# Attention in a two-layer decoder trunk: the causal mask added by rounded fp32 matmuls, a pair's first two blocks turned in one go, the head norms' small transposes held until the next turning

## Chip, core and metric

One core of one Trainium2 chip runs the whole program. The time is device microseconds from start to end of one execution; the kernel before was run three times, with a median of 1141.16 us. The engines are named as the profile names them: PE (TensorE matmul), PEld (its weight loads), DVE (VectorE), ACT (ScalarE), POOL (GpSimd), SP (the queue that issues most DMAs).

## What is computed

Two layers over 512 tokens of width 1024. The first has the attention that the change touches: 16 heads of width 64, 8 with forgetting attention (fox) and 8 with stick-breaking attention. Cut to that:

```
q, k, v = heads of rms_norm(h) @ w_in;   q, k = rms_norm(q), rms_norm(k)   # per head
# fox heads
logits = q k^T * 64**-0.5 + cum_f[query] - cum_f[key];  logits = -inf where key > query
o_fox  = softmax(logits) @ v
# stick-breaking heads
z = q k^T * 64**-0.5;  w = exp(log_sigmoid(z) + sum of log_sigmoid(-z) over later keys), strictly causal
o_sb   = w @ v
h = h + concat(o_fox, o_sb) @ w_out
```

A gated convolution mixer in the second layer and an MLP in each layer follow; the change leaves them alone.

## The kernel before

Nearly all matmuls take fp32 numbers split in two rounded halves (`hi`, and `lo`, the rest), and a product is three matmuls, hi·hi, hi·lo and lo·hi (lines 271 to 273 for the projections, 527 to 529 for the values). Each weight chunk that arrives (`raw`) is split by one ACT copy (L250) and one DVE subtraction (L251).

Heads go in 8 pairs `p` of two heads `e`; pairs 0 to 3 are fox, 4 to 7 stick-breaking. Query blocks of 128 rows go in three units: blocks 0 and 1 together, block 2, block 3 (`UNITS`). For each pair and unit:

- `logits` (L623): the **score** matmuls (L645). Head 0 lies in rows 0 to 63 of the PE array and head 1 in rows 64 to 127, each with its own PSUM bank of tag `b` (four buffers, shared with the projections). For fox pairs a fourth group with `dl` and `dr` adds the decay, and then **the mask** is added (L654): an identity matrix times a 128x128 mask, both bf16, over all 128 rows of the array. Softmax (L662 to 668) or sigmoids and a scan (L683 to 689) give the weights `w`.
- `turn` (L694): one unit later, **the turning**: transposes of 128x128 on PE into a PSUM bank of tag `c` (two buffers); L705 for blocks 0 and 1, L717 for blocks 2 and 3. ACT copies the bank to `pt` hi (L711, L720) and DVE takes the rest (L712, L721), which frees the bank.
- `weigh` (L724), when a pair's last block is turned: `w @ v` on PE (L741), then L747 and L748 join the two heads.

Between these, `fill` runs pieces of **fillers**: generators that yield matmuls of the following pairs' projections (`queries_keys`, L545), of the values, and at last of the output projection (L752, L766).

A pair's head norm is a chain of small steps off the projections, each put off by some us of planned PE time with `after` (L190) and started by `spend` (L185), which adds up planned time and runs what has come due: **sums** (L564, sums of squares over a head, matmuls 32 columns wide in the array, into a `c` bank), **turned_sums** (L572, two transposes in the same bank, which is free only after L574), the reciprocal roots on DVE (L356 to 368), and **rows** (L597, two times four transposes into two `c` banks; DVE multiplies at L599, L372 and L373 split the result into `qk_hi`, `qk_lo`). The scores of that pair need it (`need`, L540).

The order in which the program issues its instructions comes from a scheduler behind the tile framework: it takes the code's order as a wish and moves instructions of an engine where its own estimate finds the operands late. So a change in when steps are called moves rows on all engines.

Of the kernel before, what the change touches and what calls it, by code (L numbers as in the profile page):

```python
# [17 lines left out]
F32 = mybir.dt.float32  # L18
F32R = mybir.dt.float32r
# [6 lines left out]
P = 128  # L26
S = 512
# [16 lines left out]
ORDER = (1, 0, 1, 1, 1, 1, 3)  # L44
SUMS, FLAT, ROWS = 3.0, 1.5, 8.0
NSUMS, NROWS, LATE = 4.0, 3.0, 7.0
FILL1, FILL2, BEFORE = 1.5, 3.3, 2.0
UNITS = (0, 1), (2,), (3,)
CLASSIC = 3
SHARE = 0.58  # L50
# [3 lines left out]
def trunk(  # L54
# [7 lines left out]
    act, dve, pe, pool = nc.scalar, nc.vector, nc.tensor, nc.gpsimd  # L62
# [10 lines left out]
    def bank(tag):  # L73
        n_ps[0] += 1
        return ps.tile([P, S], F32, tag=tag, name=f"ps{tag}{n_ps[0]}", bufs={"a": 2, "b": 4, "c": 2}[tag])
# [52 lines left out]
    ident16 = begin[:, S - P:S]  # L128
    make_identity(nc, ident16)
    mask = const.tile([P, P], BF16, tag="mask", name="mask")  # L130
# [51 lines left out]

    clock, later, fillers, quota = [0.0], [], [], [0.0]

    def spend(us):  # L185
        clock[0] += us
        while later and later[0][0] <= clock[0]:
            later.pop(0)[2]()

# [8 lines left out]
    def fill(us):  # L198
        quota[0] += us
        while quota[0] > 0 and fillers:  # L200
            before = clock[0]
            if next(fillers[0], None) is None:
                fillers.pop(0)
            quota[0] -= clock[0] - before
# [240 lines left out]
    def choose():  # L445

        one = const.tile([P, 4, 4], F32, tag="one", name="one")
        pool.memset(one, 0.0)
        for j in range(4):
            for e in range(2):  # L450
                pool.affine_select(
                    out=one[:, j, :], in_=one[:, j, :], pattern=[[-1, 4]], compare_op=ALU.not_equal,
                    fill=1.0, base=-(e * HD + 4 * j), channel_multiplier=1,
                )
        both = const.tile([P, 2, 4], F32, tag="both", name="both")
        pool.tensor_tensor(both, one[:, 0::2, :], one[:, 1::2, :], op=ALU.add)
        two = const.tile([P, 4, 2], F32, tag="two", name="two")
        pool.tensor_tensor(two, one[:, :, 0:2], one[:, :, 2:4], op=ALU.add)
        by = const.tile([P, 4], F32, tag="by", name="by")
        pool.tensor_tensor(by, two[:, :, 0], two[:, :, 1], op=ALU.add)  # L460
        cols = const.tile([P, 4], F32, tag="cols", name="cols")
        pool.tensor_tensor(cols[:, 0:2], by[:, 0:2], by[:, 2:4], op=ALU.add)
        pool.tensor_tensor(cols[:, 2:4], by[:, 0::2], by[:, 1::2], op=ALU.add)
        pool.tensor_scalar(cols[:, 3:4], cols[:, 3:4], -1.0, None, op0=ALU.mult)
        sel = {n: cols[:, i:i + 1] for i, n in enumerate(("hi", "lo", "q", "-k"))}
        for p in range(4):
            sel["q", p], sel["k", p] = (both[:, i, p:p + 1] for i in range(2))
        return sel
# [71 lines left out]
    def need(what):  # L540
        while what not in done:
            assert fillers
            fill(0.5)
# [75 lines left out]
    def at_once(u):  # L619

        return (slice(0, 2),) if u == 0 else (slice(0, 1), slice(1, 2))

    def logits(p, u):  # L623


        fox = p < 4
        need(("qk", p))
        need("decay")
        (k_hi, k_lo), (q_hi, q_lo) = (halves[p][i] for i in range(2))
        bs = UNITS[u]  # L630
        ss = [bank("b") for _ in range(2)]

        parts, at_ = [], 0
        for i, b in enumerate(bs):
            n = (b + 1) * P
            parts.append((b, n, 256 * i, at_))
            at_ += n
            spend((4 if fox else 3) * max(n, 256) * 0.00044 + (0.12 if fox else 0))

        def scores(ql, kl, first, last):  # L640
            for b, n, c, _ in parts:
                wide = max(n, 256)
                for e in range(2):
                    rows = slice(e * HD, (e + 1) * HD)
                    pe.matmul(ss[e][:, c:c + wide], ql[rows, b * P:n], kl[rows, 0:wide], start=first and b == bs[0], stop=last and b == bs[-1])  # L645

        scores(q_hi, k_hi, True, False)
        scores(q_hi, k_lo, False, False)
        scores(q_lo, k_hi, False, not fox)
        if fox:  # L650
            scores(dl[:, p, :], dr, False, False)
            for e in range(2):
                for b, n, c, _ in parts:
                    pe.matmul(ss[e][:, c + b * P:c + n], ident16, mask, start=False, stop=b == bs[-1])  # L654
        w = aw.tile([P, 2, S], F32, tag="w", name=f"w{p}{u}", bufs=2)
        own = [w[:, :, a:a + n] for b, n, c, a in parts]
        if fox:
            m = len(bs)
            top, total, inv = (tiny.tile([P, m, 2], F32, tag=f"{t}{m}", name=f"{t}{p}{u}") for t in ("top", "total", "inv"))
            for j, (b, n, c, a) in enumerate(parts):  # L660
                for e in range(2):
                    dve.reduce_max(top[:, j, e:e + 1], ss[e][:, c:c + n], axis=AX.X, negate=True)  # L662
                    act.activation(own[j][:, e, :], ss[e][:, c:c + n], AF.Exp, bias=top[:, j, e:e + 1], accum_out=total[:, j, e:e + 1])
            for es in at_once(u):
                dve.reciprocal(inv[:, :, es], total[:, :, es])
                for j in range(m):
                    for e in range(es.start, es.stop):
                        dve.tensor_scalar(own[j][:, e, :], own[j][:, e, :], inv[:, j, e:e + 1], None, op0=ALU.mult)
        else:

            scale = q_scale[p]
            if not rests:
                rests.append(aw.tile([P, 2, S + 1], F32, tag="rest", name="rest", bufs=1))
                pool.memset(rests[0][:, :, S:S + 1], 0.0)
            rest = rests[0]
            if u == 0:
                pool.memset(rest[:, :, P:P + 1], 0.0)
            for es in at_once(u):
                for j, (b, n, c, a) in enumerate(parts):
                    end = P if b == 0 else S  # L680
                    keys = slice(end - n, end)
                    for e in range(es.start, es.stop):
                        act.activation(rest[:, e, keys], ss[e][:, c:c + n], AF.Sigmoid, scale=scale[:, 1, b, e:e + 1])  # L683
                        act.activation(own[j][:, e, :], ss[e][:, c:c + n], AF.Sigmoid, scale=scale[:, 0, b, e:e + 1])
                        back = rest[:, e, keys][:, ::-1]
                        dve.tensor_tensor_scan(back, back, begin[:, S - n:S][:, ::-1], 0.0, op0=ALU.mult, op1=ALU.max)  # L686
                for j, (b, n, c, a) in enumerate(parts):
                    end = P if b == 0 else S
                    dve.tensor_tensor(own[j][:, es], own[j][:, es], rest[:, es, end - n + 1:end + 1], op=ALU.mult)
        return [(b, x) for (b, n, c, a), x in zip(parts, own)]  # L690
# [87 lines left out]
    def output_begin():  # L778
        last_w.append([weights(), weights(AHEAD - 1)])
        yield from output_part(range(4), range(2), "b")  # L780
        last_w.append([weights(AHEAD - 1), weights(0)])
        yield from output_part(range(4), (2,), "b")
# [96 lines left out]
    aw = attn.enter_context(tc.tile_pool(name="aw", bufs=2))  # L879
# [4 lines left out]
    o_tiles = {0: mixed(0)}  # L884

    dl = ap_.tile([P, 4, S], F32R, tag="dl", name="dl")
    dr = aw.tile([P, 2, S + 1], F32, tag="rest", name="dr", bufs=1)[:, 0, 0:S].bitcast(F32R)
    sel = choose()
    run(qk0)
    load_small()  # L890
# [7 lines left out]
    units = [(p, u) for p in range(8) for u in range(len(UNITS))]  # L898
    waiting = {}
    fill(PRE)  # L900
    for g in range(len(units) + 2):
        if g < len(units):
            waiting[g] = logits(*units[g])
            fill(FILL1)
        if g == len(units):
            fillers.append(output_begin())
            fill(BEFORE)
        if g >= 2 and units[g - 2][1] == len(UNITS) - 1:
            p = units[g - 2][0]
            weigh(p)  # L910
            if p == 3:
                fillers.append(output(0, residual))
        if 1 <= g <= len(units):
            for b, w in waiting.pop(g - 1):
                turn(units[g - 1][0], b, w)
                fill(FILL2 / len(UNITS[units[g - 1][1]]))
    fill(1e9)

    def residual_out(o, acc, nxt):
# [668 lines left out]
```

## Time and profile before

| | |
|---|---|
| median of 3 runs | 1141.16 us (1140.47 to 1141.63) |
| the profiled execution | 1140.43 us, span in the profile 1138.5 us |
| mean granted clock of PE | 0.998 |
| attention by units, about 45 to 275 us | 230 us |
| PE idle in that stretch | 3.3 us |

A row of the timeline view gives start, duration, engine, line, tile written <- tiles read, rows*columns of the array, the shape that streams through, and how many instructions were merged. PE matmuls overlap in their pipeline, so what one costs is the distance from its start to the next start, not its duration.

### The profile page before, as it was taken

Reading aid. Unit: us, or ns where it says so; the run is one execution under the profiler, and the core shown is the slowest. Engines: PE = TensorE matmul, PEld = TensorE weight load, DVE = VectorE, ACT = ScalarE, POOL = GpSimd, SP = SyncE. Lnnn points to the kernel's source line nnn. Section 1 sums busy time; section 2 is a strip of 40 time slices with the busy share of each in tenths; the row PEclk is TensorE's granted clock in tenths of the full one; section 3 lists DMA queues with packets and bytes.
Section 4 is the critical chain, followed back from the end, with each engine's and each line's share of the span. In section 5 each row is a group of like instructions: output and inputs, shape, how many; then the busy total and the mean of one; then the engine's idle time right before and its main releaser. Section 6 shows DMA issues by size and latency. Waiting matters only on the chain.

```text
span 1138.5 us, 19066 instructions
## 1 busy us (share of the span) xinstructions
PE 1123.4 (99%) x7547; PEld 1006.6 (88%) x7547; DVE 959.3 (84%) x1453; ACT 669.3 (59%) x999; POOL 136.0 (12%) x150
## 2 busy tenths in 40 slices
PE   8999999999999999999999999999999999999998
PEld 6888787878889999999999899988889999998776
DVE  5787888887899899989788889865898898989775
ACT  7556576755545667676475455543445767676553
POOL 4000000000012111014400001000012111014400
PEclk9999999999999999999999999999999999999999
DMA  6412212022366877689944555543275867699952
GB/s 192 112 38 75 56 39 73 26 87 75 110 178 120 179 170 162 173 247 190 213 101 143 145 144 133 113 118 98 83 192 117 191 161 162 172 246 190 206 144 83
DMA packets 161080, 155.31 MB, mean 136 GB/s; under 512 B 6396, under 2 KB 136492, under 8 KB 160992
## 3 DMA queue, kind: packets, MB, share of 16 engines
q1 hardware_dynamic: 124256, 106.94, 30.6%
q0 software_dynamic: 36576, 47.10, 25.8%
q8 instruction: 59, 0.97, 0.3%
q14 instruction: 29, 0.24, 0.1%
q10 hardware_dynamic: 160, 0.07, 0.0%
HBM read 149.10 MB, written 2.10 MB: 133 GB/s over the span
## 4 chain that ended last, share of the span: by engine, by line
PE 86%; DVE 8%; DMA 2%; ACT 2%; issue 1%; SPq 0%; DVEq 0%; ACTq 0%
PE psb L997 25%; PE psa L997 10%; PE psb L1505 10%; PE psb L271 6%; PE psb L272 6%; PE psb L273 6%; PE psa L1505 5%; PE psa L273 4%; PE psa L272 4%; PE psa L271 4%; DVE wlo L251 2%; DMA raw<-in_ffn_w_down 2%; PE psb L645 1%; PE psa L741 1%; DVE rest L686 1%
## 5 line engine op out<-in xcount | busy, mean ns | idle before, releaser
L250 ACT ACTIVATE whi<-raw 128x1024 fp32r<-128x1024 f32 (+2 forms) x97 | 100.0, 1033 | 110.2 <-PE psb L272 32.0
L251 DVE TENSOR_TENSOR wlo<-raw,whi 128x1024 fp32r<-128x1024 f32 (+2 forms) x97 | 115.2, 1189 | 41.4 <-ACT whi L250 39.4
L997 PE MATMUL psb<-p_hi,wlo_p 128*128 128x256 f32 x384 | 108.3, 282 | 0.6 <-DVE wlo_p L950 0.6
L997 PE MATMUL psb<-p_lo,whi_p 128*128 128x256 f32 x384 | 108.1, 281 | 0.0
L997 PE MATMUL psb<-p_hi,whi_p 128*128 128x256 f32 x384 | 107.8, 281 | 0.0
L271 PE MATMUL psb<-hs_a,whi 128*128 128x512 f32 x256 | 104.6, 409 | 0.0
L273 PE MATMUL psb<-hs_a,wlo 128*128 128x512 f32 x256 | 101.3, 397 | 0.0
L997 PEld LDWEIGHTS psb<-p_hi,wlo_p 128*128 128x128 f32 x384 | 72.2, 188 | 0.8 <-DVE wlo_p L950 0.8
L997 PEld LDWEIGHTS psb<-p_hi,whi_p 128*128 128x128 f32 x384 | 72.8, 190 | 0.0
L997 PEld LDWEIGHTS psb<-p_lo,whi_p 128*128 128x128 f32 x384 | 72.2, 188 | 0.0
L997 PE MATMUL psa<-p_lo,whi_p 128*128 128x256 f32 x256 | 72.0, 281 | 0.0
L997 PE MATMUL psb<-q_hi,whi_q 128*128 128x256 f32 x256 | 72.0, 281 | 0.0
L997 PE MATMUL psb<-q_lo,whi_q 128*128 128x256 f32 x256 | 72.0, 281 | 0.0
L997 PE MATMUL psb<-q_hi,wlo_q 128*128 128x256 f32 x256 | 72.0, 281 | 0.0
L997 PE MATMUL psa<-p_hi,wlo_p 128*128 128x256 f32 x256 | 72.0, 281 | 0.0
L997 PE MATMUL psa<-p_hi,whi_p 128*128 128x256 f32 x256 | 71.8, 281 | 0.0
L1505 PE MATMUL psb<-act,whi 128*128 128x256 f32 x352 | 63.0, 282 | 0.4 <-DVE act L950 0.4
L380 DVE SCALAR_TENSOR_TENSOR uv<-yv,taps,uv 128x511 f32<-128x511 f32 (+1 forms) x88 | 62.5, 745 | 0.2
L380 DVE SCALAR_TENSOR_TENSOR ug<-yg,taps,ug 128x511 f32<-128x511 f32 (+1 forms) x88 | 62.0, 743 | 0.3 <-ACT ug L377 0.3
L271 PEld LDWEIGHTS psb<-hs_a,whi 128*128 128x128 f32 x256 | 48.4, 189 | 10.7 <-issue 1.2
L273 PEld LDWEIGHTS psb<-hs_a,wlo 128*128 128x128 f32 x256 | 48.1, 188 | 10.9
L1505 PE MATMUL psb<-whi,act 128*128 128x512 f32 x176 | 57.4, 399 | 0.1
(453 smaller groups left out, 3654.9 us busy)
## 6 DMA issues: line engine op xcount, KB each, us to landing
raw<-in_attn_w_in SPq DMA_DIRECT2D x24, 512.0 KB, 4.0
raw<-in_ffn_w_up SPq DMA_DIRECT2D x24, 512.0 KB, 3.9
raw<-in_ffn_w_down SPq DMA_DIRECT2D x20, 512.0 KB, 8.1
X<-in_ffn_w_up SPq DMA_DIRECT2D x16, 512.0 KB, 4.7
W<-in_ffn_w_up SPq DMA_DIRECT2D x16, 512.0 KB, 6.7
Y<-in_ffn_w_up SPq DMA_DIRECT2D x16, 512.0 KB, 4.6
Z<-in_ffn_w_up SPq DMA_DIRECT2D x16, 512.0 KB, 4.9
Y<-in_ffn_w_up POOLq DMA_DIRECT2D x16, 512.0 KB, 9.8
```

What stands on the lines that cost most here:

```text
L250: return (act.activation(hi[:, at_], raw[:, at_], AF.Copy), dve.tensor_tensor(lo[:, at_], raw[:, at_], f32(hi[:, at_]), op=ALU.subtract))
L251: dve.tensor_tensor(lo[:, at_], raw[:, at_], f32(hi[:, at_]), op=ALU.subtract))
L271: made = [pe.matmul(acc, w[0], rhs[0], start=first, stop=False), pe.matmul(acc, w[0], rhs[1], start=False, stop=False), pe.matmul(acc, w[1 ...
L272: pe.matmul(acc, w[0], rhs[1], start=False, stop=False),
L273: pe.matmul(acc, w[1], rhs[0], start=False, stop=last)]
L380: dve.scalar_tensor_tensor(dst[:, d:], src[:, 0:S - d], tap(j), dst[:, d:], op0=ALU.mult, op1=ALU.add)
L645: pe.matmul(ss[e][:, c:c + wide], ql[rows, b * P:n], kl[rows, 0:wide], start=first and b == bs[0], stop=last and b == bs[-1])
L686: dve.tensor_tensor_scan(back, back, begin[:, S - n:S][:, ::-1], 0.0, op0=ALU.mult, op1=ALU.max)
L741: pe.matmul(out_, w, t[:, first:first + step * (NB - k - 1) + 1:step, :], start=k == 0 and i == 0, stop=k == NB - 1 and i == 1)
L997: pe.matmul(to, w[a][:, k, c], x[b][:, k, :], start=fresh and i + k + t == 0, stop=i == 1 and k == 3 and t == 2, skip_group_check=not fresh)
L1505: pe.matmul(to, l, r, start=begin and o + t == 0, stop=end and t == 2 and o == (0 if layer else 1), skip_group_check=not fresh)
```

## The change

Three edits:

1. **The mask's operands.** Two 128x128 tiles of rounded fp32, `above` (the mask) and `unit` (the identity), are made by two POOL copies in the spare second half of the tile that holds `dr`. The 32 mask matmuls read these instead of the bf16 ones.
2. **Blocks 0 and 1 of a pair are turned one behind the other**, and `fill(FILL2)` follows once; before, half of it stood behind each.
3. **The put-off steps are held.** While units run, `spend` starts a step only when it is `GRACE` = 4.0 us overdue; a new `gather`, called ahead of each turning, starts all that are due at all. So sums, turned_sums and rows come in front of a turning, or 4 us late.

```
+    grace = [0.0]
     def spend(us):
         clock[0] += us
+        while later and later[0][0] + grace[0] <= clock[0]:
+            later.pop(0)[2]()
+
+    def gather():
         while later and later[0][0] <= clock[0]:
             later.pop(0)[2]()
...
-                    pe.matmul(ss[e][:, c + b * P:c + n], ident16, mask, start=False, stop=b == bs[-1])
+                    pe.matmul(ss[e][:, c + b * P:c + n], unit, above, start=False, stop=b == bs[-1])
...
+    held_rows = aw.tile([P, 2, S + 1], F32, tag="rest", name="dr", bufs=1)
+    dr, above, unit = (held_rows[:, i, c:c + n].bitcast(F32R) for i, c, n in ((0, 0, S), (1, 0, P), (1, P, P)))
+    pool.tensor_copy(above, mask)
+    pool.tensor_copy(unit, ident16)
...
+    grace[0] = GRACE
     for g in range(len(units) + 2):
...
         if 1 <= g <= len(units):
+            gather()
             for b, w in waiting.pop(g - 1):
                 turn(units[g - 1][0], b, w)
-                fill(FILL2 / len(UNITS[units[g - 1][1]]))
+            fill(FILL2)
+    grace[0] = 0.0
     fill(1e9)
```

In the changed file the lines below 190 stand 6 lower (scores L651, mask L660, sums L570, turned_sums L578, rows L603, turning L711 and L723). What the edits do to the order of instructions is seen at two places.

**Pair 3, block 3, on PE.** `psb_...` are the two heads' score banks. Before, the rows alternate between the heads, and each mask matmul has a weight load of its own in the program (rounded fp32 matmuls carry theirs):

```order
L645 MATMUL psb_1878<-qk_hi_1634,qk_hi_1645 128x512
L645 MATMUL psb_1879<-qk_hi_1634,qk_hi_1645 128x512
L645 MATMUL psb_1878<-qk_lo_1635,qk_hi_1645 128x512
L645 MATMUL psb_1879<-qk_lo_1635,qk_hi_1645 128x512
L645 MATMUL psb_1878<-qk_hi_1634,qk_lo_1646 128x512
L645 MATMUL psb_1879<-qk_hi_1634,qk_lo_1646 128x512
L645 MATMUL psb_1878<-dr,dl 128x512
L645 MATMUL psb_1879<-dr,dl 128x512
L654 LDWEIGHTS begin
L654 MATMUL psb_1878<-mask,begin 128x128
L654 LDWEIGHTS begin
L654 MATMUL psb_1879<-mask,begin 128x128
```

In the changed order the same unit stands so, between products of the values:

```order
L535 MATMUL psb_1978<-whi_1608,hs_a_117 128x256
L651 MATMUL psb_1985<-qk_hi_1660,qk_hi_1671 128x512
L651 MATMUL psb_1985<-qk_lo_1661,qk_hi_1671 128x512
L651 MATMUL psb_1985<-qk_hi_1660,qk_lo_1672 128x512
L651 MATMUL psb_1985<-dr,dl 128x512
L660 MATMUL psb_1985<-dr 128x128
L651 MATMUL psb_1986<-qk_hi_1660,qk_hi_1671 128x512
L651 MATMUL psb_1986<-qk_lo_1661,qk_hi_1671 128x512
L651 MATMUL psb_1986<-qk_hi_1660,qk_lo_1672 128x512
L651 MATMUL psb_1986<-dr,dl 128x512
L660 MATMUL psb_1986<-dr 128x128
L533 MATMUL psb_1978<-whi_1608,hs_a_117 128x256
```

Head 0's rows and its mask are now complete before head 1's begin.

**Pair 1, from its rows to its first scores.** Before, on PE, `rows` of pair 1 (L597) stands among fillers, ahead of the turning of pair 0's block 2, and 18 more value products follow the last row shown before pair 1's first score:

```order
L597 MATMUL psc_923<-ident,qwide_818 128x128 x4
L597 MATMUL psc_934<-ident,qwide_820 128x128 x4
L271 MATMUL psb_864<-hs_a_117,whi_682 128x512
L272 MATMUL psb_864<-hs_b_118,whi_682 128x512
L273 MATMUL psb_864<-hs_a_117,wlo_683 128x512
L717 MATMUL psc_945<-ident,w_832 128x128 x3
L527 MATMUL psb_971<-whi_719,hs_a_117 128x256
L528 MATMUL psb_971<-wlo_720,hs_a_117 128x256
L529 MATMUL psb_971<-whi_719,hs_a_117 128x256
L717 MATMUL psc_951<-ident,w_832 128x128 x3
```

In the changed order it is held until the turning of block 3; its second half (`psc_1070`) stands eight value products behind its first (`psc_1059`):

```order
L603 MATMUL psc_1070<-ident,qwide_920 128x128 x4
L535 MATMUL psb_1043<-whi_844,hs_b_118 128x256
L578 MATMUL psc_1024<-ident,flat_1033 128x128 x2
L723 MATMUL psc_1179<-ident,w_874 128x128 x4
L651 MATMUL psb_1081<-qk_hi_1066,qk_hi_1077 128x256
L651 MATMUL psb_1082<-qk_hi_1066,qk_hi_1077 128x256
L651 MATMUL psb_1081<-qk_hi_1066,qk_hi_1077 128x256
L651 MATMUL psb_1082<-qk_hi_1066,qk_hi_1077 128x256
L651 MATMUL psb_1081<-qk_lo_1067,qk_hi_1077 128x256
L651 MATMUL psb_1082<-qk_lo_1067,qk_hi_1077 128x256
```

And this is what DVE has queued there in the changed order, from the product with the first `rows` bank to the last half that pair 1's scores read:

```order
L605 TENSOR_TENSOR qn_1064<-qk_681,psc_1059 128x512
L257 TENSOR_TENSOR wlo_1135<-raw_1136,whi_1134 128x1024
L605 TENSOR_TENSOR qn_1075<-qk_716,psc_1070 128x512
L379 TENSOR_TENSOR qk_lo_1067<-qn_1064,qk_hi_1066 128x512
L527 SCALAR_TENSOR_TENSOR v_950<-psb_1043,ncol_n_330,v_950 128x4x64
L257 TENSOR_TENSOR wlo_1141<-raw_1142,whi_1140 128x1024
L379 TENSOR_TENSOR qk_lo_1078<-qn_1075,qk_hi_1077 128x512
```

The distance from `rows` to the scores that read its result has shrunk from 18 and more products to one product and six transposes.

Counted over the whole PE order of attention, the scores of the 24 units stand in 27 unbroken pieces before and in 32 in the change. The array's division (all 128 rows; halves of 64 rows for the scores; 32 columns for the sums) changes from one matmul to the next 68 times before and 82 times in the change. Score matmuls of the two heads that do not alternate amount to one pair of them before (384 wide) and seven in the change (512 wide).

More of the change, by code (lines that the diff above doesn't have):

```diff
@@ L46 @@
 NSUMS, NROWS, LATE = 4.0, 3.0, 7.0
-FILL1, FILL2, BEFORE = 1.5, 3.3, 2.0
+FILL1, FILL2, BEFORE, GRACE = 1.5, 3.3, 2.0, 4.0
 UNITS = (0, 1), (2,), (3,)
@@ L886, in trunk @@
     dl = ap_.tile([P, 4, S], F32R, tag="dl", name="dl")
-    dr = aw.tile([P, 2, S + 1], F32, tag="rest", name="dr", bufs=1)[:, 0, 0:S].bitcast(F32R)
+    held_rows = aw.tile([P, 2, S + 1], F32, tag="rest", name="dr", bufs=1)
+    dr, above, unit = (held_rows[:, i, c:c + n].bitcast(F32R) for i, c, n in ((0, 0, S), (1, 0, P), (1, P, P)))
+    pool.tensor_copy(above, mask)
+    pool.tensor_copy(unit, ident16)
     sel = choose()
```

## The prediction

> **What bounds the kernel now.** First the page's busy times, then the stretch of attention among the windows of the trace, then who waits there for whom, for PE.
>
> ```profile
> PE 1123.4 (99%) x7547; PEld 1006.6 (88%) x7547; DVE 959.3 (84%) x1453; ACT 669.3 (59%) x999; POOL 136.0 (12%) x150
> 45.00:275.00 230.00, 226.71 (x1484) 185.69 (x1483) 189.73 (x410) 143.18 (x294) 0.45 (x5) 1.00 0.22 60
> ```
>
> PE is busy for 99% of the span, and in attention for 226.71 of 230.00 us. So PE sets the time there, and PE stands idle for 3.3 us in all: whatever this change does to waits, it cannot win more than that. DVE has 189.73 us of work in the stretch, near enough to be late now and then. DMA's share is 0.22, so transfers don't matter here. The clock is granted in full.
>
> ```profile
> PE psc L597 <- DVE pt L721: 1.3, 1, 1.3
> PE psc L564 <- DVE pt L721: 1.1, 2, 0.7
> PE psa L741 <- DVE o L748: 0.5, 1, 0.5
> PE psa L741 <- DVE h L787: 0.2, 1, 0.2
> ```
>
> These are PE's waits in attention (us in total, times, longest). 2.4 us of the 3.3 are of one kind: a put-off step (rows, L597, or sums, L564) wants a `c` bank while DVE has not yet emptied it of a turning (L721). That is the wait which holding the steps until the next turning can remove.
>
> What a busy PE does not show is how densely it works. Here is the timeline of PE around the scores of a stick-breaking unit inside a stream of projections:
>
> ```profile
> 166.40 0.40 PE L273 MATMUL psb<-hs_a,wlo 128*128 128x512 f32 x1
> 166.73 0.50 PE L645 MATMUL psb<-qk_hi,qk_hi 64*128 64x512 f32 x2
> 167.07 0.39 PE L645 MATMUL psb<-qk_lo,qk_hi 64*128 64x512 f32 x2
> 167.29 0.40 PE L645 MATMUL psb<-qk_hi,qk_lo 64*128 64x512 f32 x2
> 167.63 0.50 PE L271 MATMUL psb<-hs_a,whi 128*128 128x512 f32 x1
> 167.96 0.40 PE L272 MATMUL psb<-hs_a,whi 128*128 128x512 f32 x1
> 168.19 0.40 PE L273 MATMUL psb<-hs_a,wlo 128*128 128x512 f32 x1
> ```
>
> Two things are to be seen. A pair of 512-wide scores, one per head, takes 167.29 - 167.07 = 0.22 us, no more than one 512-wide product (168.19 - 167.96 = 0.23): the heads run side by side. And each change between 128 rows and 64 rows costs twice: the last step before it takes 0.33 and the first after it 0.34, where 0.22 to 0.23 is the rule. On the way in 0.10 + 0.12, on the way out 0.11 + 0.10. **A change of the array's division costs 0.21 us.** No wait for another engine explains it; the profile calls such gaps "issue", and in attention they are the weight loader's longest entry:
>
> ```profile
> PEld psb L645 <- issue: 4.9, 17, 0.4
> ```
>
> **The mask (edit 1).** PE at a fox unit of one block (two masks) and of two blocks (four):
>
> ```profile
> 142.54 0.39 PE L645 MATMUL psb<-dr,dl 64*128 64x512 f32 x2
> 142.86 0.28 PE L654 MATMUL psb<-mask,begin 128*128 128x128 bf16 x2
> 142.96 0.48 PE L271 MATMUL psb<-hs_a,whi 128*128 128x512 f32 x1
> 143.28 0.40 PE L272 MATMUL psb<-hs_b,whi 128*128 128x512 f32 x1
> ...
> 53.54 0.40 PE L654 MATMUL psb<-mask,begin 128*128 128x128 bf16 x4
> 53.75 0.48 PE L271 MATMUL psb<-hs_a,whi 128*128 128x512 f32 x1
> ```
>
> From the last scores to the second product behind is 143.28 - 142.54 = 0.74 us; without masks, above, it is 167.96 - 167.29 = 0.67. Two bf16 masks cost 0.07. Four take 0.21 where two take 0.10, so they cost 0.18. With eight units of two and four of four, all masks cost 8 x 0.07 + 4 x 0.18 = 1.3 us. The change of division is paid with or without them, so rounded operands save none of it; that excludes a gain beyond the 1.3 itself.
>
> No rounded mask is in the trace. The nearest rows are 128-wide rounded matmuls (the last step of `weigh`, two of them, then a 512-wide one) and 128-wide fp32 transposes, each with a fresh load of 128 columns:
>
> ```profile
> 160.19 0.62 PE L741 MATMUL psa<-pt,v 128*128 128x128 f32 x3
> 160.25 0.56 PE L741 MATMUL psa<-pt,v 128*128 128x128 f32 x2
> 160.37 0.44 PE L741 MATMUL psa<-pt,v 128*128 128x512 f32 x1
> ...
> 58.95 0.38 PE L705 MATMUL psc<-ident,w 128*128 128x128 f32 x2
> 59.09 0.48 PE L271 MATMUL psb<-hs_a,whi 128*128 128x512 f32 x1
> 59.40 0.40 PE L272 MATMUL psb<-hs_a,whi 128*128 128x512 f32 x1
> ...
> 144.46 0.81 PE L717 MATMUL psc<-ident,w 128*128 128x128 f32 x6
> 145.03 0.48 PE L271 MATMUL psb<-hs_a,whi 128*128 128x512 f32 x1
> 145.34 0.40 PE L272 MATMUL psb<-hs_b,whi 128*128 128x512 f32 x1
> ```
>
> The rounded ones take 0.06 and 0.12. Transposes: 59.40 - 58.95 = 0.45, less 0.23 for the product behind, is 0.11 each. I take 0.11 for a mask, since masks come back to back with a load each, as transposes do: 32 x 0.11 = 3.5, against 1.3 now. **Edit 1 costs +2.2 us**; with 0.06 each it is +0.6, and I keep +2.5 (0.12 each) as the upper end.
>
> ```profile
> L654 PEld LDWEIGHTS <-begin x32: 95/98/99, 53.5 to 142.9; 128*128 128x128 bf16 x32
> L741 PEld LDWEIGHTS psa<-pt,v x128: 186/188/192, 82.0 to 258.1; 128*128 128x128 f32 x128
> ```
>
> A bf16 load has 98 ns in the trace, a rounded one 188. [...]
>
> **Turning in one go (edit 2).** Six transposes in one burst: 145.34 - 144.46 = 0.88, less 0.23, is again 0.11 each. A burst of two and one of six cost the same per transpose, so interrupting a stream has no fee of its own, and drawing two bursts together saves nothing on PE: 0.
>
> **The held steps (edit 3), and the order that follows.** Nothing is added or removed; instructions move, and what moves costs changes of division and broken pairs. From the counts of the order:
> - The division changes 82 times, not 68: 14 x 0.21 = **+2.9 us**. Scores now stand in 32 pieces, because their banks or operands come late in the scheduler's plan; and sums, which stood next to scores three times (one change shared), no longer do.
> - Seven pairs of 512-wide scores no longer alternate between heads, against one 384-wide before; each that runs alone takes 0.23 more per pair: 7 x 0.23 - 0.17 = **+1.4 us**.
> - The waits of rows and sums for DVE's L721 go, since at the next turning the last one's banks have long been emptied: **-2.4 us**, at least 0. What is late next is the step's own user.
> - That user is worked out for pair 1, where the new order leaves least room. Durations:
>
> ```profile
> L599 DVE TENSOR_TENSOR qn<-qk,psc 128x512 f32<-128x512 f32 x10 | 6.7, 680 | 1.0 <-PE psc L597 0.9
> L372 ACT ACTIVATE qk_hi<-qn 128x512 fp32r<-128x512 f32 x10 | 6.2, 628 | 9.0 <-DVE qn L599 9.0
> L251 DVE TENSOR_TENSOR wlo<-raw,whi 128x1024 fp32r<-128x1024 f32 x27 | 32.9, 1218 | 6.0 <-ACT whi L250 5.6 <-PE psb L529 0.2
> ```
>
> PE gets from the start of the second rows (`psc_1070`) to pair 1's first score in ten transposes and a product, 10 x 0.11 + 0.12 = 1.2 us. The score needs `qk_hi_1077`. The first rows began 0.44 + 8 x 0.12 = 1.4 us earlier and were done about 0.8 us before our start; then DVE has the product (0.68), the weight half queued behind it (1.22) and the second product (0.68), which ends at about 1.8; ACT's half (0.63) makes 2.4. PE waits 2.4 - 1.2 = 1.2 us. The last half, `qk_lo_1078`, has another 1.22 in front of it, which PE partly covers with three products: up to 0.9 more. **+1.5 us**, between 0 (DVE finds the weight not yet there and the product goes first in time) and 2.1. Queued behind the waiting score are the turning and the next unit's scores, so it is paid in full.
> - Sums and turned_sums share one `c` bank, and in the new order turnings stand between them (at six of the seven pairs, counted in the order). One bank is left for the turning then, and its second half waits for ACT and DVE; the scheduler put fillers there as cover. I take 0, and 3 us for the case that this cover is too thin.
> - Steps that run in `gather` no longer count against the fillers' quota, so the fillers are used up sooner. At the end three products stand between the last turning and the product with the values, where there were fifteen.
>
> ```profile
> 251.48 1.03 PE L717 MATMUL psc<-ident,w 128*128 128x128 f32 x8
> 252.74 1.29 DVE L721 TENSOR_TENSOR pt<-psc,pt 128x512 fp32r<-128x512 f32 x2 [1.41 <-ACT pt L720]
> ```
>
> The last half of `pt` was ready 252.74 + 1.29 - 251.48 = 2.55 us after the turning began. PE will be there after 8 x 0.11 + 3 x 0.23 = 1.6 us, and has up to 1.0 us to wait; the order puts the first hi products ahead, so I take half: **+0.5 us**.
>
> POOL's two copies stand at about 5 us, where `dr`'s memory is free and nothing of POOL's is waited for: 0.
>
> **Sum:** 2.2 + 2.9 + 1.4 - 2.4 + 1.5 + 0.5 = **+6.1 us**. The profiled execution (1140.43, span 1138.5) becomes 1146.5; it lay 0.7 under the median of 1141.16, so in medians I say **1147.3 us**, 0.5% slower.
>
> **The rivals.**
> - *Not slower: DVE's lateness is what counts, and the held steps cure it.* All 3.3 us of idle time vanish, pair 1 finds its halves ready, and the changes of division fall where PE would have waited anyhow. Then only the mask is left, at its low end: 1141.2 - 3.3 + 0.6 = 1138.5. For it: 2.4 of 3.1 us are the wait aimed at. Against it: 0.21 us is paid on every excursion, also where nothing waits (at 166 us above), so the 2.9 + 1.4 are work and not waiting. It decides as long as less than 2.7 of those 4.3 us show up (3.3 - 0.6). Chance 0.10.
> - *About the same: half of it.* The pieces of scores stand where DVE is late in truth, so the 3.3 us of idle time are used up by them, and the mask takes 0.06 each. 1141.2 + 2.9 + 1.4 + 0.6 - 3.3 = 1142.8. Chance 0.15.
> - *Worse: the shared `c` bank.* The turning's second half waits at six pairs for 0.5 us on average, and the old waits stay in another place: 1147.3 + 3 + 1.2 = 1151.5. For it: DVE is at 189.73 of 230 us. Chance 0.15.
>
> My forecast has 0.60. The low end of the range takes in the cases down to about no change, the high end the third rival. A measurement of this kernel can tell about 0.2% (2.3 us) from no change: faster by more 0.10, within 0.13, slower by more 0.77.
>
> **What would show it.** In the changed kernel's profile: mask matmuls about 0.11 us apart, with loads of some 188 ns; the unit of pair 3, block 3, with scores of one head 0.23 us apart; PE's waits on L721 at rows and sums gone, and a wait of a score on ACT's `qk_hi` near 70 us; PE's idle time in attention near 3 us and its stretch some 6 us longer, all else of the same length. I am wrong if attention is no longer than before, or if the idle time grows by more than the moved work.

## The result, and the profile after

The change makes the kernel slower: **1148.19 us** (median of five runs, 1147.22 to 1152.91) against 1141.16 us (five runs by then, 1139.70 to 1141.63), a ratio of 1.0076 with an interval of 1.0051 to 1.0100. The profiled execution took 1148.19 us, its span 1146.0 us. The forecast, 1147.3, was near; its terms were not all right, and that is what the experiments were for.

The page's row of busy times, and the windows' row of attention, which now ends some 7 us later (columns as before):

```profile
PE 1128.9 (99%) x7547; PEld 1008.7 (88%) x7547; DVE 959.6 (84%) x1453; ACT 670.1 (58%) x999; POOL 136.4 (12%) x152
45.00:282.00 237.00, 231.47 (x1478) 187.06 (x1477) 187.61 (x407) 142.01 (x290) 0.44 (x5) 1.00 0.20 57
```

PE is idle for 237.00 - 231.47 = 5.5 us of attention, where it was 3.3. The other engines' busy times stand nearly as they did. The first product of the next stage (L997, now L1009) starts at 355.23 us and not at 346.95: **+8.3 us arise in attention**. At the end 7.5 are left (spans 1146.0 and 1138.5). Behind attention PE is idle for 9.1 us, 0.8 more than before (8.3); but the kernel before has a stretch there at half the granted clock (0.51, third from the end of its row), which is worth 3.50 x 0.49 = 1.7 us:

```profile
567.50:571.00 3.50, 3.50 (x19) 3.50 (x18) 1.35 (x2) 2.23 (x3) 0.00 (x0) 0.51 1.10 262
```

The changed kernel's profile has no such stretch: its clock is 1.00 in the same window, and in every 20 us up to 1140 us.

Of the 8.3 us, 2.2 are idle time and about 6.0 are PE working longer on the same 7547 matmuls. Taken by lines (from start to next start, waits taken off, from 45 us to the next stage), the rows of the masks are 2.8 us longer, the scores 2.2, all transposes together 0.2 and the rest 0.6. PE's waits in that stretch:

```profile
PE psb L533 <- DVE v L527: 1.7, 1, 1.7
PE psa L747 <- DVE h L793: 1.6, 1, 1.6
PE psc L723 <- DVE qn L605: 0.7, 1, 0.7
PE psb L651 <- ACT qk_hi L378: 0.7, 1, 0.7
PE psc L711 <- DVE qn L605: 0.4, 1, 0.4
PE psc L723 <- DVE pt L727: 0.3, 1, 0.3
```

The waits of rows and sums for the turning's L721 (2.4 us before) are gone, as the prediction had it. But two waits that it did not have stand at the top, 1.7 and 1.6 us in one piece each: for the copy of the values out of PSUM (L527), and for the sum with the residual (L793). Both are DVE's.

Why was DVE late? These are rows of its queue, and one each of ACT and PE, around the first of the two (start, duration, engine, line, operation, tiles; rows in between are left out):

```profile
204.29 1.22 DVE L257 TENSOR_TENSOR wlo<-raw,whi 128x1024 fp32r<-128x1024 f32 x1
204.59 0.48 ACT L526 ACTIVATE v<-psb,ncol_n 128x256 fp32r<-128x256 f32 x1 [0.49 <-PE psb L535]
205.43 0.17 DVE L374 SCALAR_TENSOR_TENSOR qr<-rb_qk,ry_qk 128x16 f32<-128x16 f32 x1
205.51 0.68 DVE L379 TENSOR_TENSOR o_lo<-o,o_hi 128x512 fp32r<-128x512 f32 x1
...
206.26 0.42 DVE L596 COPY qwide<-qr 128x512 f32<-128x512 f32 x1
206.60 0.48 DVE L527 SCALAR_TENSOR_TENSOR v<-psb,ncol_n,v 128x256 fp32r<-128x256 f32 x1
207.13 0.39 PE L533 MATMUL psb<-whi,hs_a 128*128 128x256 f32 x1 [1.69 <-DVE v L527]
```

ACT had its half of the values done at 205.07. DVE came to the other half only at 206.60. In front of it stood the end of a weight half (L257), the split of the heads' output (L379, `o_lo`), and the last links of a head norm's roots (`qr`, `qwide`); PE's next products waited for the bank. So the put-off chain has a share in this wait, beside DVE's other work.

In front of the second one, the sum with the residual, DVE's row has two scans and two products of the stick-breaking weights, and no step of a head norm:

```profile
226.09 1.80 DVE L692 TENSOR_TENSOR_SCAN rest<-rest,begin 128x384 f32<-128x384 f32 x2
227.80 1.00 DVE L695 TENSOR_TENSOR w<-w,rest 128x384 f32<-128x384 f32 x2
228.72 0.68 DVE L793 TENSOR_TENSOR h<-psa,h 128x512 f32<-128x512 f32 x1
```

Why the changed order brings these together is not shown.

The masks, at a unit with two and one with four (PE; a row merges the instructions that are alike):

```profile
127.99 0.39 PE L651 MATMUL psb<-dr,dl 64*128 64x512 f32 x2
128.31 0.44 PE L660 MATMUL psb<-dr 128*128 128x128 f32 x2
128.59 0.44 PE L277 MATMUL psb<-hs_a,whi 128*128 128x512 f32 x1
128.87 0.39 PE L278 MATMUL psb<-hs_a,whi 128*128 128x512 f32 x1
...
110.47 0.66 PE L660 MATMUL psb<-dr 128*128 128x128 f32 x4
110.97 0.45 PE L277 MATMUL psb<-hs_a,whi 128*128 128x512 f32 x1
...
L660 PEld LDWEIGHTS psb<-dr x32: 186/189/192, 52.7 to 157.6; 128*128 128x128 f32 x32
```

From the scores to the second product behind is 128.87 - 127.99 = 0.88 us, where two bf16 masks took 0.74; four take 110.97 - 110.47 = 0.50, where they took 0.21. The loads have a median of 189 ns. With eight units of two and four of four, that is 8 x 0.14 + 4 x 0.29 = 2.3 us.

Three smaller predictions, each in PE's timeline: pair 3, block 3, where one head's scores now follow one another; pair 1's turning and first score; and the last turning with the product with the values.

```profile
155.44 0.39 PE L651 MATMUL psb<-qk_lo,qk_hi 64*128 64x512 f32 x1
155.68 0.39 PE L651 MATMUL psb<-qk_hi,qk_lo 64*128 64x512 f32 x1
155.91 0.38 PE L651 MATMUL psb<-dr,dl 64*128 64x512 f32 x1
...
81.95 0.66 PE L723 MATMUL psc<-ident,w 128*128 128x128 f32 x4 [0.73 <-DVE qn L605]
83.28 0.50 PE L651 MATMUL psb<-qk_hi,qk_hi 64*128 64x256 f32 x4 [0.68 <-ACT qk_hi L378]
...
268.50 1.03 PE L723 MATMUL psc<-ident,w 128*128 128x128 f32 x8
...
270.07 2.74 PE L747 MATMUL psa<-pt,v 128*128 128x512 f32 x16
```

A score alone takes 0.23 to 0.24 us, as long as two side by side. Pair 1 waits 0.73 + 0.68 = 1.4 us. The tail doesn't wait: PE begins the product with the values 1.6 us after the last turning began. DVE ends the last half of `pt` only at 271.05 us, 2.55 us after it, as late as before; the sixteen products run until 272.65, and those that need the last half come late enough.

### The profile page after: what moved, and what is told of

The parts are those of the page before. It is cut to its first block, busy times and chain, and to the rows that moved or that the text cites. A ratio compares the mean times of both kernels' runs of the same rounds, so it can differ in the third digit from the quotient of the medians.

```text
span 1146.0 us, 19069 instructions
## 1 busy us (share of the span) xinstructions
PE 1128.9 (99%) x7547; PEld 1008.7 (88%) x7547; DVE 959.6 (84%) x1453; ACT 670.1 (58%) x999; POOL 136.4 (12%) x152
## 4 chain that ended last, share of the span: by engine, by line
PE 87%; DVE 6%; DMA 3%; ACT 2%; issue 1%; DVEq 0%; ACTq 0%; POOLq 0%
PE psb L1009 24%; PE psb L1517 10%; PE psa L1009 9%; PE psb L277 6%; PE psb L279 6%; PE psb L278 6%; PE psa L1517 5%; PE psa L277 4%; PE psa L279 4%; PE psa L278 4%; PE psb L651 2%; DMA raw<-in_ffn_w_down 2%; DVE wlo L257 2%; PE psa L747 1%; PE psc L723 1%
## 5 line engine op out<-in xcount | busy, mean ns | idle before, releaser
L257 DVE TENSOR_TENSOR wlo<-raw,whi 128x1024 fp32r<-128x1024 f32 (+2 forms) x97 | 115.3, 1190 | 40.8 <-ACT whi L256 40.4
L1009 PE MATMUL psb<-p_hi,wlo_p 128*128 128x256 f32 x384 | 108.2, 282 | 0.0
L1009 PE MATMUL psb<-p_lo,whi_p 128*128 128x256 f32 x384 | 108.1, 281 | 0.0
L1009 PE MATMUL psb<-p_hi,whi_p 128*128 128x256 f32 x384 | 107.8, 281 | 0.0
L1009 PEld LDWEIGHTS psb<-p_hi,whi_p 128*128 128x128 f32 x384 | 72.8, 190 | 0.0
L1009 PEld LDWEIGHTS psb<-p_lo,whi_p 128*128 128x128 f32 x384 | 72.3, 188 | 0.0
L1009 PE MATMUL psb<-q_hi,wlo_q 128*128 128x256 f32 x256 | 72.1, 282 | 0.1
L1009 PEld LDWEIGHTS psb<-p_hi,wlo_p 128*128 128x128 f32 x384 | 72.2, 188 | 0.0
L1009 PE MATMUL psa<-p_hi,wlo_p 128*128 128x256 f32 x256 | 72.1, 282 | 0.0
L1009 PE MATMUL psb<-q_lo,whi_q 128*128 128x256 f32 x256 | 72.0, 281 | 0.0
L1009 PE MATMUL psa<-p_lo,whi_p 128*128 128x256 f32 x256 | 72.0, 281 | 0.0
L1009 PE MATMUL psb<-q_hi,whi_q 128*128 128x256 f32 x256 | 71.9, 281 | 0.0
L1009 PE MATMUL psa<-p_hi,whi_p 128*128 128x256 f32 x256 | 71.8, 281 | 0.0
```

The source lines that it names most:

```text
L257: dve.tensor_tensor(lo[:, at_], raw[:, at_], f32(hi[:, at_]), op=ALU.subtract))
L1009: pe.matmul(to, w[a][:, k, c], x[b][:, k, :], start=fresh and i + k + t == 0, stop=i == 1 and k == 3 and t == 2, skip_group_check=not fresh)
```

## The experiments

Three theories were to be told apart. **Work:** the changes of the array's division, the broken pairs and the masks are the cost. **Lateness:** the held head norms end later than their users need them, and what DVE and PE then do out of step is the cost. **Bank:** sums, held in a `c` bank until a turning has passed, starve the turnings. Each kernel was timed against the kernel before on its own chip, whose medians lay between 1140.7 and 1140.9 us. "Changes" and "broken pairs" are counted in PE's order as in the change's section (before 68 and 0.75, the change 82 and 7, in units of a 512-wide pair).

### Each edit alone

Edit 1, the masks alone:

```
-                    pe.matmul(ss[e][:, c + b * P:c + n], ident16, mask, start=False, stop=b == bs[-1])
+                    pe.matmul(ss[e][:, c + b * P:c + n], unit, above, start=False, stop=b == bs[-1])
...
+    pool.tensor_copy(above, mask)
+    pool.tensor_copy(unit, ident16)
```

> Edit 1 alone (rounded masks, everything else as before). The prediction's price, 0.11 us per rounded mask for 0.04 per bf16 one, gives +2.2 us; the order has one change of division more (69 for 68) and no broken pair, about 0 together. So about 1143.3 us, PE idle time in attention as before (3.3 us). A rival that holds the mask for free because attention has waits to hide it in: 1141.2 us, with less idle time.

Measured: 1142.97 us, ratio 1.0020 (1.0011 to 1.0029), +2.2 us. The next stage starts 2.4 us later, of which 0.3 is idle time; so PE's own work grew by 2.1 us. A mask's weight load has a median of 189 ns in rounded fp32 (L660, in the changed kernel's rows above) and of 98 ns in bf16 (L654, the kernel before).

Edit 2, one fill behind both turnings:

```
             for b, w in waiting.pop(g - 1):
                 turn(units[g - 1][0], b, w)
-                fill(FILL2 / len(UNITS[units[g - 1][1]]))
+            fill(FILL2)
```

> Edit 2 alone (one fill behind both blocks). No fee for a burst of transposes, so only the order counts: two changes of division more (70) and one more broken pair (2 x 0.21 + 0.23 = 0.6 us): about 1141.8 us. A rival that gives each burst of transposes a fee of its own: eight bursts fewer, 8 x 0.1 to 0.2, so about 1140 us.

Measured: 1144.37 us, ratio 1.0033 (1.0021 to 1.0046), +3.6 us: **a miss.** PE's waits for a `c` bank in this kernel:

```profile
PE psc L597 <- DVE pt L721: 1.8, 2, 1.3
PE psc L705 <- DVE qn L599: 1.3, 1, 1.3
PE psc L564 <- DVE pt L721: 1.3, 2, 0.7
```

The second row is new: a turning waits 1.3 us for a bank that `rows` filled and DVE has not read. It is the second block's turning, at 165.40 us; six value products stand in front of it. At the same place in the kernel before, fifteen do, and nothing waits. So the fill between the two turnings was time in which DVE emptied banks. PE's idle time in attention is 5.4 us where it was 3.3, which is 2.1 of the 3.6 us. That transposes cost the same in long and short bursts was right, and it was not the question.

Edit 3, the held steps alone, and edits 2 and 3 together with the bf16 masks:

```
+        while later and later[0][0] + grace[0] <= clock[0]:
+            later.pop(0)[2]()
+
+    def gather():
...
+    grace[0] = GRACE
...
+            gather()
```

> Edit 3 alone (held steps, bf16 masks, two fills). By the counts of the order: 84 changes of division for 68 (+3.4 us), 8.5 broken pairs for 0.75 (+1.8 us), waits as in the changed kernel (5.4 for 3.1 us, +2.3): 1146.4 without, 1148.7 us with the waits. The rival that it is the waits alone: +2.3 us, 1143.5, with PE's idle time grown by all of the difference.

> Edits 2 and 3 without 1 (the changed kernel with bf16 masks). If edit 1 adds by itself, this lies 2.2 us under the changed kernel: about 1146 us; by the counts 82 changes (+2.9) and 8.5 broken pairs (+1.8) and 2.3 of waits make +7.0. If the mask was hidden in waits, this is as slow as the changed kernel, 1148 us.

Measured: 1146.6 us, ratio 1.0058 (1.0045 to 1.0070), and 1146.58 us, ratio 1.0054 (1.0041 to 1.0066). So edit 3 alone costs 5.8 us, and edit 2 on top of it nothing. Edit 1 on top of both brings 1.2 more: the change is 7.0 us over its own kernel before, and the two without the mask 5.8. For edit 3 the counts and the waits together made 1148.7, and the counts alone 1146.4: the median is at the lower one, though PE's idle time did grow, to 5.3 us. Alone the three sum to 2.2 + 3.6 + 5.8 = 11.6, together they cost 7.0: edits 2 and 3 are not two costs. A reason may be that with the steps in front of the turning nothing comes between the two turnings that the fill had to cover; no run shows that by itself.

### Is a change of division work?

28 matmuls are added to the projections of pairs 1 to 7 of the kernel before. They add zeros (the output stays). In one kernel they use 64 rows of the array, so that each makes two changes of division; in the other all 128, so that none does:

```
+            for k, made in enumerate(products(acc, weights())):
+                if p and k in (2, 4):
+                    pe.matmul(acc[:, 0:P], begin[0:HD, 0:P], begin[0:HD, 0:P], start=False, stop=False)
+                yield made
```

(`begin[0:P, 0:P]` in the other.)

> The kernel before with 28 more matmuls, two inside each query or key projection of pairs 1 to 7, that add zeros times zeros (bf16, 128 wide) to the running sum and use 64 rows of the array. Each makes two changes of division: 28 x (2 x 0.21 + 0.05) = +13.2 us, about 1154 us. If the 0.21 us is a matter of scores waiting and not of the division, only the matmuls themselves count: +1.4 us, 1142.

> The control: the same 28 matmuls over all 128 rows, so no change of division. As bf16 masks cost 0.04 to 0.05 us each: +1.4 us, about 1142.2. If a change of type in the stream costs like a change of division, as much as the kernel with 64 rows.

Measured: 1149.6 us, ratio 1.0074 (1.0059 to 1.0089), and 1143.9 us, ratio 1.0024 (1.0013 to 1.0036). PE's timeline at one inserted matmul (L607), on 64 rows and then on 128:

```profile
62.80 0.40 PE L273 MATMUL psb<-hs_a,wlo 128*128 128x512 f32 x1
63.13 0.23 PE L607 MATMUL psb<-begin 64*128 64x128 bf16 x1
63.28 0.50 PE L271 MATMUL psb<-hs_a,whi 128*128 128x512 f32 x1
63.62 0.39 PE L272 MATMUL psb<-hs_a,whi 128*128 128x512 f32 x1
```

```profile
61.78 0.40 PE L273 MATMUL psb<-hs_a,wlo 128*128 128x512 f32 x1
62.02 0.23 PE L607 MATMUL psb<-begin 128*128 128x128 bf16 x1
62.05 0.48 PE L271 MATMUL psb<-hs_a,whi 128*128 128x512 f32 x1
62.37 0.40 PE L272 MATMUL psb<-hs_a,whi 128*128 128x512 f32 x1
```

The excursion to 64 rows takes 63.62 - 62.80 = 0.82 us, the same matmul on all rows 62.37 - 61.78 = 0.59. Two changes are worth 0.23 us here, and by the medians (1149.6 - 1143.9) / 28 = 0.20. The first kernel came out 4 us under what was expected, the second 2 us over. **So a change of division is PE's own time**, with no wait anywhere near. But it is 0.10 to 0.12 each, half of the 0.21 read at the scores: the product behind the small matmul is 0.09 late (0.32 and not 0.23) in the second timeline too, where nothing was divided. Whether that 0.09 comes from the bf16 type, from the narrow matmul or from its load, no run tells; between rounded fp32 matmuls the price may be the whole 0.21.

### Which held step costs

`after` gets a flag, and only flagged steps are held:

```
-        while later and later[0][0] <= clock[0]:
+            due = [e for e in later if e[0] + (grace[0] if e[3] else 0.0) <= clock[0]]
...
+            after(ROWS, lambda: rows(wides), True)
```

That is rows alone. In the second kernel sums and turned_sums carry the flag, in a third sums alone.

> Edit 3 for the rows alone: sums and turned_sums start when due, bf16 masks and two fills as before. The order has 65 changes of division (68 before) and 1.5 broken pairs (0.75): 3 x 0.21 - 0.17 = -0.5 us, and the 1.3 us that rows waited for L721 may go as well: 1139 to 1140.3 us. If holding the rows is what makes the scores late (the wait worked out for pair 1), it is slower by some 1.5 us: 1142.3.

> Edit 3 for sums and turned_sums alone, rows when due. 71 changes for 68 and 3.75 broken pairs for 0.75: +0.6 + 0.7 = +1.3 us; the shared bank, held across turnings, may add waits: 1142.1 us without, 1144 with 2 us of them. If the long hold of the bank were free, the 1.1 us that sums waited for L721 would go: 1141.

Measured: holding rows gives 1140.76 us, ratio 1.0003 (0.9994 to 1.0012), no difference (1139 to 1140.3 were expected). Holding sums and turned_sums gives 1146.53 us, ratio 1.0052 (1.0040 to 1.0065): **holding these two costs as much as the whole of edit 3.** It is a miss, since 1142.1 to 1144 were expected. With 71 changes and 3.75 broken pairs, work alone would be 3 x 0.21 + 3 x 0.23 = 1.3 us. PE's idle time in attention grew from 3.3 to 6.2 us, which makes 4.2 with the work; 5.8 were measured, so 1.6 us stay open. The clock doesn't explain them: the two runs at a mean clock of 1.000 took 1145.28 and 1146.30 us. PE's longest waits, rows held first, then sums:

```profile
PE psc L727 <- DVE qn L609: 2.3, 2, 1.2
PE psa L751 <- DVE h L797: 0.3, 1, 0.3
```

```profile
PE psc L727 <- DVE qn L609: 2.1, 2, 1.9
PE psc L607 <- DVE pt L731: 1.3, 1, 1.3
PE psa L751 <- DVE h L797: 1.1, 1, 1.1
```

In the first, the waits of rows and sums for the turning (2.4 us) have become a wait of the turning for rows (2.3): both are about the same two banks, and turning the order round turns the wait round. In the second the old wait is still there (1.3), with the new ones beside it.

Is it the bank that the held sums occupy? The same kernel with sums in a bank of tag `a`; and, against "the two transposes come too late", sums held but turned_sums not:

```
-            t = bank("c")
+            t = bank("a")
```

> As the run that holds sums and turned_sums alone (1146.5 us), but their shared PSUM bank is taken from tag a and not from c, so that the turnings in between keep both c banks. If the cost of holding comes from the c bank that is kept across turnings, most of the 5.8 us goes: 69 changes and 3.75 broken pairs are +0.9 us, so about 1141.6. If it comes from the head norms being late for the scores, the bank makes no difference: 1146.5.

> Holds sums alone; turned_sums follow when due, so that the c bank is kept for one turning at most, at four of eight pairs. By the counts 74 changes for 68 (+1.3 us) and 2.5 broken pairs for 0.75 (+0.4): 1142.4 us. If it is the lateness of the head norms that costs, nearly as much as with both held: 1145 or more.

Measured: 1146.85 us, ratio 1.0049 (1.0035 to 1.0063), and 1144.98 us, ratio 1.0034 (1.0021 to 1.0047). With another bank nothing is won, so **the bank theory falls**: it isn't the sums that starve the turnings. PE's turnings and rows still wait for each other's `c` banks there, 3.8 us in all. With sums held and turned_sums free, 4.1 of the 5.8 us remain. PE's longest waits in this last kernel:

```profile
PE psb L655 <- ACT qk_hi L382: 1.7, 4, 0.6
PE psc L607 <- DVE pt L731: 1.0, 2, 0.6
PE psa L751 <- DVE h L797: 0.9, 1, 0.9
```

Scores wait four times for ACT's `qk_hi`, which no score does in the kernel before. Sums are the first link of the chain that ends there; holding them makes the whole head norm late, while rows, held alone, are covered. That fits the lateness theory, which is left by exclusion. It is not shown to be the whole cause: where turned_sums are held too, no wait of a score for `qk_hi` is listed. There pair 1's rows start at 73.9 us, 8.0 later than before, and its first score at 77.2, 6.4 later; in the code, `need` runs fillers until the rows have been called. So the scores moved with the rows, and the waits stand at other tiles: turnings, rows, the residual's sum. No run made the chain less late, with a smaller `GRACE` for instance, to see the cost go.

### Are the scattered scores the cost?

The change, with scores and masks kept in the order in which the code writes them:

```
-                    pe.matmul(ss[e][:, c:c + wide], ql[rows, b * P:n], kl[rows, 0:wide], start=first and b == bs[0], stop=last and b == bs[-1])
+                    tc.keep_in_program_order(pe.matmul(ss[e][:, c:c + wide], ql[rows, b * P:n], kl[rows, 0:wide], start=first and b == bs[0], stop=last and b == bs[-1]))
...
+                    tc.keep_in_program_order(pe.matmul(ss[e][:, c + b * P:c + n], unit, above, start=False, stop=b == bs[-1]))
```

> The changed kernel with its scores and masks told to stay in the order in which the code writes them. The order then has 76 changes of division for 82 and 2 broken pairs for 7. If these are PE's own work, as the prediction counts, they take 6 x 0.21 + 5 x 0.23 = 2.4 us off: about 1145.8 us where the changed kernel has 1148.2. If the pieces only fill time in which PE would wait for DVE, the time stays at 1148.2 and PE's idle time in attention grows by 2.4 us (from 5.5).

Measured: 1150.53 us (four runs), ratio 1.0083 (1.0069 to 1.0097): not faster than the change. The work did shrink: with 76 changes and 2 broken pairs the scores' distances from start to start sum to 1.7 us less than in the change. But PE waits 0.9 us more (a new 1.0 us of L747 for DVE's `o`, L754), and after its longest wait the clock falls to half. The window holds most of that stretch:

```profile
207.00:210.40 3.40, 3.38 (x29) 2.74 (x30) 3.30 (x4) 1.23 (x4) 0.00 (x0) 0.63 0.40 135
```

A granted clock of 0.63 in 3.40 us is worth 1.3 us; the stretch itself begins at 207.8 us and is worth 1.7. Two more such stretches stand in the MLPs (granted clock 0.91 over 560 to 580 us, and again over 1080 to 1100). All four runs had a mean clock of 0.994 to 0.998, so the total doesn't say what whole units are worth; the scores' own term does, and it fell about as counted (6 x 0.21 + 5 x 0.23 = 2.4 expected). The scores themselves wait no longer than in the change (0.7 us for `qk_hi`); the new wait is the product with the values'. Whether late operands are why the scheduler had cut the units is not shown.

### The opposite of holding

The kernel before, with one word changed: sums take a bank of tag `a`, so that the two `c` banks are left to rows and turnings.

```
-            t = bank("c")
+            t = bank("a")
```

> The kernel before with one word changed: the sums take their PSUM bank from tag a. The order has 63 changes of division for 68 (-1.0 us) and nothing of sums waits for L721 any more (-1.1 us): 1138.6 us, a gain on both kernels. If the sums now wait for, or hold up, the product with the values and the output projection, which use the a banks, the gain is lost: 1141 or more.

Measured: **1138.56 us, ratio 0.9977 (0.9966 to 0.9988)**, 2.3 us faster than the kernel before and faster than every other kernel here. The windows' row of attention and all of PE's listed waits in it:

```profile
45.00:282.00 237.00, 235.73 (x1527) 193.61 (x1526) 199.63 (x425) 149.64 (x304) 0.44 (x5) 1.00 0.22 61
PE psc L597 <- DVE pt L721: 0.6, 1, 0.6
PE psa L741 <- DVE o L748: 0.5, 1, 0.5
PE psa L741 <- DVE h L787: 0.2, 1, 0.2
```

PE is idle for 1.3 us. The waits for L721 have shrunk from 2.4 us to 0.6, and the order has 63 changes of division instead of 68. The next stage starts 3.3 us earlier: 2.0 are idle time, and 1.3 are work, where five changes at 0.21 make 1.0. So most of the wait that the change aims at could be had out of the way, with a bank and not with time: the step `rows` of pairs 1 to 7 starts 0.6 to 3.2 us earlier here, and none later.

## Why the prediction was right, and where not

**Right in sum: +7.0 us against +6.1.** By its steps:

- *The mask, +2.2.* Right: +2.2 measured alone (2.1 of it PE's work), 0.11 us per mask in the timeline.
- *Changes of division and broken pairs, +2.9 + 1.4 = 4.3.* About right in sum: the work in attention grew by 6.0 us, less the mask's 2.1 leaves 3.9, and of these 2.2 stand at the scores themselves. That a division costs PE time without any wait was tested apart and holds; the test's price is 0.10 to 0.12, and why the scores show 0.21 is open. Scores alone at 0.23 us came out to the digit. Keeping the units whole took the scores' 1.7 us back, but not the time.
- *Waits of rows and sums gone, -2.4.* Right as far as it went: they are gone.
- *Pair 1, +1.5.* Right in size (1.4 us), in part at another place: half of it is the turning that waits for DVE's first product (`qn`), half the score.
- *The tail, +0.5.* Wrong: no wait. `pt` was as late as predicted, but the order put enough of the sixteen products ahead; the chosen half of 1.0 us should have been 0.
- *Turning in one go, 0.* **This step failed when taken alone** (+3.6): it asked what bursts cost on PE, and not what the filler between two turnings covers. Beside edit 3 it did come to nothing.
- *The shared bank, 0, with 3 us kept as a rival.* The 0 was right for the bank; the rival's mechanism fell (1146.85 with another bank, 1146.53 without; both with rows not held).

**The failed term is the sum of the waits.** By the steps it was -2.4 + 1.5 + 0.5 = -0.4; measured was +2.2. The prediction followed the held step to its own first user, and stopped there. The two longest new waits stand elsewhere, 1.7 us at the values' copy and 1.6 us at the residual's sum, for steps of DVE that only share a queue with the head norm. "What is late next" was asked for PE and the chain, and not for DVE's other customers. This term was 2.6 us too low, the moved work 0.4 too high, and behind attention 0.8 us came back; so a sum of 6.1 stands beside 7.5 in the spans and 7.0 in the medians. The 0.8 is luck: it is about what the stretch of half the clock in the kernel before (1.7 us) leaves over 0.8 us of longer waits. In attention, where the change is, the sum lies 2.2 us off.

Of the rivals, the faster one assumed that DVE's lateness is what counts and that holding cures it. The waits that it wanted cured were cured, and others took their place; rows held alone (1140.76) show that at its plainest, 2.4 us of wait exchanged for 2.3. Holding the sums is what undid the case. The rival had pair 1's halves ready in time; its first score waited 0.7 us for `qk_hi`. Not settled: by which way the held sums bring the two longest waits; 1.6 of the 5.8 us that holding them costs; why edits 2 and 3 don't add up; and what the change would be with sums left unheld in an `a` bank and rows held, which was not tried.

## What to carry to other kernels

Here a wait for a buffer between two busy engines was not removed by moving one user in time: it came back on the other user (2.4 us as 2.3, with rows held), or on a third one that shares the late engine's queue (1.7 and 1.6 us in the change). So try first to give one user a buffer of another pool; here one word did that, and took most of the wait away (2.4 us to 0.6). And read a batch of moved instructions on the receiving engine's queue, not only along their own chain.

## What the runs showed of the hardware

**A wait of PE can cost twice.** The granted clock falls to one half (0.50 in the second row here, 0.51 in the kernel before from 567.5 us on) for about 3.4 us at a time, and in these traces, as long as PE has work, it does so within 1.2 us of a wait. These are two windows of the kernel with sums held (columns as before: PE's busy time comes first, the granted clock third from the end):

```profile
229.40:232.80 3.40, 1.55 (x9) 1.05 (x8) 3.40 (x6) 1.20 (x3) 0.10 (x1) 1.00 0.17 65
232.80:236.20 3.40, 3.40 (x18) 2.45 (x16) 2.63 (x4) 0.84 (x1) 0.00 (x0) 0.50 0.00 0
```

In the first window PE stands for 3.40 - 1.55 = 1.85 us, in the wait for DVE that leads that kernel's list above; in the next it runs at 0.50, which takes 3.40 x 0.50 = 1.7 us of work away. Over all fourteen profiles, attention has such a stretch four times, always behind a wait of 1.65 to 1.85 us in one piece, and never where the longest wait is 1.3; in the MLPs it follows two waits of 1.45 to 3.5 us together. Not every such wait brings one: the change's own profile has waits of 1.7 and 1.6 us in attention and a clock of 1.00 throughout. That is also the likely source of its spread: the runs of 1147.22 and 1148.19 had a mean clock of 1.000, those of 1151.57 and 1152.91 of 0.994 and 0.995, and 0.005 of 1146 us is 5.7 us. Where in those two runs the clock fell was not recorded.

PE need not stand still for all of the time ahead of the fall: in the first window it worked for 1.55 of 3.40 us, and the next ran at 0.50. That the wait brings the fall is read from this order; why one wait is followed by half the clock and another of the same length is not, no run shows.

**A division of the array is not free in a stream.** Entering and leaving 64 rows costs 0.20 to 0.23 us with a bf16 matmul between rounded fp32 ones, and 0.43 around the rounded fp32 scores (in the prediction's rows at 166 us: 0.33 + 0.34 + 0.34 + 0.33, less four times 0.22 to 0.23).
